# The first stage in written order, with the conditioning matrix taken in four eighth pairs of scale and shift

## The chip, the cores and the metric

The kernel runs on one core of a Trainium2 chip. The metric is device time in microseconds (us) of one execution; less is better. A core has five engines with instruction streams of their own: TensorE (PE, the matmuls), VectorE (DVE), ScalarE (ACT), GpSimd (POOL) and SyncE (SP, which here only issues DMA transfers). Each engine runs its stream in order. An instruction waits for semaphores of other engines or of DMA transfers, and everything behind it on the same engine waits with it.

## The reference

One layer of a hybrid encoder on 2048 tokens of width 1024, all float32:

```
mod = silu(c) @ w_ada + b_ada                # w_ada 1024 x 3072
shift, scale, gate = split(mod, 3)
h = RMSNorm(x) * norm_w * (1 + scale) + shift
proj = h @ w_in + b_in                       # 1024 x 4624
na = neighbourhood_attention(q, k, v, rpb) * silu(z)
ml = bidirectional chunked mLSTM(conv(q, k), v, gates) * ...
y  = concat(na, ml) @ w_out
out = RMSNorm(x + gate * y) * final_norm_w
```

The change touches `mod`, `h` and the first two column blocks of `proj`; a helper for reciprocal square roots that the later parts use too changes with it.

## The kernel before

**Numbers.** Each operand of the projection is kept as a rounded part `hi` and a remainder `lo` in a float32 form that PE multiplies in one pass. A product is three matmuls: `hi*hi`, `hi*lo`, `lo*hi`. The normed and modulated tokens stand transposed, channels on partitions, in `hhi[g]` and `hlo[g]`, one pair for each of four groups g of 512 tokens; each has eight slices k of 128 channels. A weight block is 256 columns of `w_in`. It comes as two raw halves (`raw_w`, 512 KB each); ACT writes the rounded part `whi` and POOL the remainder `wlo`. There are two slots of weights, `a` and `b`. Block 0 carries 16 more columns for the gates (`rg`).

**The first stage** is `start()`. It loads `x` of group 0, squares it on ACT (L234), takes the reciprocal root with three Newton steps (`rsqrt`, four operations a step at L1243 to L1246; for the first group on POOL, later on DVE) and scales `x` on ACT (L239). `w_ada` comes in quarters of 512 columns in the order scale 0, shift 0, scale 1, shift 1, each as eight slices of 128 rows (`wada`, 256 KB each, seven buffers). DVE multiplies every slice by a column of silu(c) and adds it up in `acc` (L249 first slice, L251 the rest). Per quarter PE sums over the partitions with four matmuls of one column against `ones` (L257). The result goes to `shT` and `gT`, the shift and the gain per channel: a copy on ACT (L260) and up to three small operations on POOL (L261, L265, L266), or one on DVE (L263).

With `gT` and `shT` of the first four slices there, `first_h` makes h of group 0: PE has transposed `x` (L273), ACT writes `hhi` and an unrounded copy `h` (L280), POOL subtracts them to `hlo` (L281). For slices 4 to 7 ACT works in two steps, `scaled` (L285) and `shifted` (L290), and DVE writes `hlo` (L291).

**The first block.** `vo_first` (L499 to L508) multiplies one slice k at a time, for all four token tiles of the group: 4 x 3 matmuls of 272 columns, into four PSUM tiles `pvo`, so that PE can start when the first slice of h is there. `vo_group` adds the biases on DVE (L524, L526), applies a sigmoid (ACT L528) and stores. With `first` unset `vo_group` does the products itself, a token tile at a time, 24 matmuls of 256 columns (`mm3`, L454 to L456). Group 0 to 2 use `vo_first` for block 0, group 3 does not; block 1 goes a tile at a time.

**What sets the order.** The work is written group by group, with generators (`next_h` as `self.chain`) that place the h of the next group (`make_h`: transposes L298, `hhi` on ACT, `h` on DVE L302, `hlo` on POOL L303) between the tiles of this one. The order in the streams then comes from a scheduler that the tile framework runs over the whole program, with its own costs; pools of buffers add waits. The streams after `start()`, blocks 2 to 5 (`tok_blocks`), convolution, mLSTM, attention and output projection, are written in the same way.

After block 5 comes the convolution stage (`pc`, first matmul at L454 from another caller). Its first products take PSUM buffers that DVE must have emptied, in L489 (`stv<-pv,brow`), which writes into staging tiles that an earlier store `d_vna` (SP, L493) must have read. SP issues that store in its stream between loads of `dec` tiles (L728), which wait for their own buffers.

## Time and profile before

| quantity | us |
|---|---|
| runs before | 1358.46, 1360.39, 1357.08 (median 1358.46) |
| the profiled execution, its own time | 1361.21 |
| its span in the trace | 1359.4 |
| mean granted TensorE clock over the span | 0.988 |
| PE busy | 1288.3 (95% of the span) |
| DVE busy | 799.0 |
| ACT busy | 532.9 |
| POOL busy | 288.9 |
| first matmul of the projection begins at | 32.21 |
| the fifth token tile of block 2 begins at | 168.09 |

The time of an execution is a little longer than its span (1361.21 against 1359.4), and a single profiled execution lies a little above the median of the runs. PE is busy nearly all the time, so a change pays if it removes time in which PE waits or runs at a lower granted clock, and the rows to look for are PE's waits and what ended them. The page's second part gives one digit per fortieth of the span, here 34 us each; the whole first stage up to block 2 lies in the first five digits.

### The profile page before, as it was taken

What the parts mean: (1) busy time and instruction counts of PE and PEld (TensorE: products, weight loads), DVE (VectorE), ACT (ScalarE), POOL (GpSimd) and SP (SyncE); (2) the same over time, 40 slices, a digit from 0 to 9 for tenths busy, and PEclk for the clock granted to TensorE, in tenths of its full rate; (3) what the DMA queues carried; (4) which work ended last, traced back from release to release, by engine and by line L of the source; (5) the groups of instructions that cost most, each with busy time, mean ns of one, the idle gap of its engine ahead of it and who ended that gap; (6) DMA issues with size and microseconds to landing.
All of it is one profiled execution on the core that took longest, in us unless ns stands there. A gap on an engine that the chain in (4) does not pass through costs nothing.

```text
span 1359.4 us, 23245 instructions
## 1 busy us (share of the span) xinstructions
PE 1288.3 (95%) x8204; PEld 1106.1 (81%) x8204; DVE 799.0 (59%) x2436; ACT 532.9 (39%) x1169; POOL 288.9 (21%) x322
## 2 busy tenths in 40 slices
PE   2989899999899999999999999899999999999996
PEld 2989899999688778788878888788877777778775
DVE  6683623111164569347677888867636676666664
ACT  4642213344432233222423333323346555555552
POOL 4454301335301011001212102212202211212121
PEclk9999999999899999999999999999999999999998
DMA  9799543599856685644665767656688986868871
GB/s 315 230 282 238 193 105 99 124 234 234 214 123 198 142 204 160 184 111 126 189 183 173 231 195 213 211 166 192 189 252 230 217 210 179 187 175 192 202 184 47
DMA packets 236359, 255.90 MB, mean 188 GB/s; under 512 B 31047, under 2 KB 192071, under 8 KB 236243
## 3 DMA queue, kind: packets, MB, share of 16 engines
q1 hardware_dynamic: 153310, 183.00, 49.8%
q0 software_dynamic: 20496, 36.21, 11.1%
q10 hardware_dynamic: 62436, 35.20, 9.2%
q8 instruction: 65, 1.06, 0.3%
q14 instruction: 52, 0.42, 0.1%
HBM read 169.81 MB, written 92.72 MB: 193 GB/s over the span
## 4 chain that ended last, share of the span: by engine, by line
PE 44%; DMA 8%; issue 6%; DVE 5%; ACT 1%; POOL 1%; SPq 0%; DVEq 0%; POOLq 0%; ACTq 0%
PE pq L892 18%; PE y L1472 9%; DMA tab<-d_t 5%; PE pT L1412 2%; PE pO L1427 2%; PE pS L1384 2%; PE px L1131 2%; PE pi L1133 2%; PE pc L454 2%; PE pc L455 2%; PE pc L456 2%; PE dc L1071 1%; DMA hlo<-d_wo 1%; PE a L1118 1%; DVE st L1055 1%
## 5 line engine op out<-in xcount | busy, mean ns | idle before, releaser
L892 PE MATMUL pq<-hhi,whi_a 128*128 128x512 f32 x512 | 208.7, 408 | 0.8 <-ACT u L797 0.8
L892 PE MATMUL pq<-hlo,whi_a 128*128 128x512 f32 x512 | 209.2, 409 | 0.0
L892 PE MATMUL pq<-hhi,wlo_a 128*128 128x512 f32 x512 | 206.9, 404 | 0.0
L892 PEld LDWEIGHTS pq<-hhi,whi_a 128*128 128x128 f32 x512 | 97.2, 190 | 17.8 <-ACT u L797 1.2
L892 PEld LDWEIGHTS pq<-hlo,whi_a 128*128 128x128 f32 x512 | 97.1, 190 | 16.2 <-issue 0.5
L892 PEld LDWEIGHTS pq<-hhi,wlo_a 128*128 128x128 f32 x512 | 97.0, 189 | 16.2
L1414 ACT ACTIVATE pt<-pT 96x384 f32<-96x384 f32 (+3 forms) x128 | 65.8, 514 | 84.7 <-PE pT L1412 81.9
L1393 ACT ACTIVATE pbuf<-pbuf,mn 128x480 f32<-128x480 f32 (+5 forms) x128 | 76.1, 596 | 54.0 <-DVE mn L1392 53.9
L1472 PE MATMUL y<-hhi,whi_a 128*128 128x512 f32 x256 | 91.6, 419 | 0.5 <-ACT whi_a L1442 0.5
L1472 PE MATMUL y<-hhi,wlo_a 128*128 128x512 f32 (+1 forms) x272 | 90.7, 399 | 0.2 <-ACT y L1479 0.2
L1392 DVE CUSTOM_DVE_ANT_0 pbuf<-pS,tab 128x480 f32<-128x480 f32 (+5 forms) x128 | 63.1, 541 | 40.3 <-PE pS L1384 29.4
L866 POOL TENSOR_TENSOR wlo_a<-rawq,whi_a 128x1024 fp32r<-128x1024 f32 x20 | 48.5, 2426 | 157.9 <-ACT whi_a L865 104.2
L1155 POOL TENSOR_TENSOR hm<-hm,ck 128x128 f32<-128x128 f32 x64 | 26.4, 412 | 253.5 <-DVE hm L1154 210.9
L1136 ACT ACTIVATE num<-px,gtile 128x129 f32<-128x129 f32 x120 | 38.2, 364 | 104.5 <-PE px L1131 83.4
L1412 PEld LDWEIGHTS pT<-ident,pbuf 128*128 128x128 f32 (+2 forms) x416 | 50.9, 137 | 29.6 <-issue 9.8
L1412 PE MATMUL pT<-ident,pbuf 128*128 128x128 f32 (+2 forms) x416 | 67.2, 275 | 8.1 <-DVE pbuf L1404 6.6
L454 PE MATMUL pvo<-whi_b,hhi 128*128 128x256 f32 x256 | 74.2, 290 | 0.6 <-DVE gates L526 0.6
L524 DVE TENSOR_TENSOR stvo<-pvo,brow 128x256 f32<-128x256 f32 x64 | 26.4, 421 | 81.6 <-PE pvo L456 62.9
L456 PE MATMUL pvo<-whi_b,hlo 128*128 128x256 f32 x256 | 72.9, 285 | 0.0
L455 PE MATMUL pvo<-wlo_b,hhi 128*128 128x256 f32 x256 | 72.8, 284 | 0.0
L739 ACT ACTIVATE dec<-dec,gtile 128x128 f32<-128x128 f32 x128 | 42.6, 393 | 56.9 <-POOL dec L732 52.9
L489 DVE TENSOR_TENSOR stv<-pv,brow 128x256 f32<-128x256 f32 x32 | 12.9, 423 | 84.4 <-PE pv L456 47.8
(301 smaller groups left out, 3484.1 us busy)
## 6 DMA issues: line engine op xcount, KB each, us to landing
ck<-d_ck SPq DMA_DIRECT2D x64, 384.5 KB
rawq<-in_w_main_dram SPq DMA_DIRECT2D x28, 512.0 KB
raw<-in_w_main_dram SPq DMA_DIRECT2D x20, 512.0 KB
d_ck<-stvo SPq DMA_DIRECT2D x16, 514.0 KB
kv<-d_ck SPq DMA_DIRECT2D x64, 128.5 KB
x<-in_x_dram SPq DMA_DIRECT2D x16, 512.0 KB
wada<-in_w_ada_dram SPq DMA_DIRECT2D x32, 256.0 KB
dec<-d_mneg SPq DMA_DIRECT2D x32, 256.0 KB
```

The costliest lines, as they stand in the source:

```text
L454: nc.tensor.matmul(ps, lhi(k), rhi(k), start=(k == 0), stop=False)
L455: nc.tensor.matmul(ps, lhi(k), rlo(k), start=False, stop=False)
L456: self.mark = nc.tensor.matmul(ps, llo(k), rhi(k), start=False, stop=(k == KT - 1))
L739: nc.scalar.activation(t[:, o, :], t[:, o, :], AF.Exp, bias=self.cols["g"][:, d, h, c : c + 1])
L866: nc.gpsimd.tensor_tensor(lo[:, :, cs], raw, hi[:, :, cs].bitcast(F32), ALU.subtract)
L892: self.mark = nc.tensor.matmul(patch_ps(ps) if patch else ps, w, self.htok(h, g, k, patch), start=(k == 0 and n == 0), stop=(k == KT - 1 a ...
L1136: nc.scalar.activation(num[:, d, :], px[:, d, :], AF.Copy, scale=self.cols["inter"][:, d, h, c : c + 1])
L1392: nc.vector.tensor_tensor_reduce(pt[:, :nk], ps, tabs[place[u]][j][:, :nk], 1.0, 3e38, ALU.add, ALU.min, mn)
L1393: nc.scalar.activation(pt[:, :nk], pt[:, :nk], AF.Exp, bias=mn, scale=-1.0, accum_out=sums[:, j : j + 1])
L1412: nc.tensor.transpose(ps[:cs, i, :], U[u][j][:, i * cs : (i + 1) * cs], self.ident)
L1414: nc.scalar.activation(t[:cs, :nch, :], ps[:cs, :nch, :], AF.Copy)
L1472: nc.tensor.matmul(y, m[:, k, :], w[k][:, cs], start=(k == 4 and n == 0), stop=(k == 3 and n == 2))
```

## The change

`start()` is run in the order in which it is written (`manual_schedule`), no longer in the scheduler's, and it is rewritten:

- `w_ada` comes in four eighth pairs e: a tile holds 256 columns of shift and the same 256 of scale for one slice of rows (128 x 2 x 256, the same 256 KB, twelve buffers). One pair gives shift and gain of two slices k = 2e and 2e+1 of h. `b_ada` is laid out to match.
- Some slices are multiplied by PE itself (`direct`: slices 1, 3, 5 of pair 0, slice 1 of pairs 1 and 2, slices 1 and 3 of pair 3); DVE sums the rest. PE adds the bias by a product with the identity that opens the group (`opened`), and the sums by four products with `ones` (`total`). `gT` is then one operation on DVE and `shT` one copy on ACT (`columns`).
- The first reciprocal root runs on DVE. The remainders of block 0's weights, of the second half of block 1's, and of h of group 0 are written by DVE, no longer by POOL.
- Twelve products into a PSUM tile `dense` that nothing reads stand in the front of PE's stream.
- All of `x` is loaded early; `x` of groups 1 and 2 lies in the memory that later holds `hhi2` and `hhi3`. `c`, `b_ada` and `norm_w` are loaded by ACT's queue.
- `vo_first` serves all four groups. It does the eight products with `hhi` for the four token tiles first and then the four with `hlo`. `make_h` of slices 0 to 4 of the next group comes in block 1 of this one, slices 5 to 7 inside the next `vo_first`.
- The fills of the attention tables are spread over the groups; a small scaling (`scale_bias`) moves back.
- `rsqrt` takes three operations per Newton step, not four, everywhere.

The diff:

```diff
-        self.start(left)
+        with self.tc.manual_schedule():
+            self.start(left)
...
+        def ada_load(e, kt):
+            w = sums[e, kt] = ada.tile([P, 2, 256], F32, tag="wada", bufs=12, name=f"wada_{e}_{kt}")
+            src = self.w_ada[kt * P : (kt + 1) * P, 0 : 2 * D].rearrange("p (a c) -> p a c", a=2)
+            nc.sync.dma_start(w, src[:, :, e * 256 : (e + 1) * 256])
+
+        def added(e, left, right):
             for j in range(4):
...
+                left_tile = left[:, j // 2, (j % 2) * P : (j % 2 + 1) * P]
+                groups[e] -= 1
+                nc.tensor.matmul(mods[e][:, j : j + 1], left_tile, right, start=False, stop=groups[e] == 0)
+
+        def opened(e):
+            groups[e] = 4 * (1 + len(direct[e]))
+            mods[e] = self.sp.tile([P, 4], F32, tag="sp", name=f"mod_{e}")
+            nc.tensor.matmul(mods[e], self.ident, bias[:, 4 * e : 4 * e + 4], start=True, stop=False)
+
+        def summed(e, kt):
+            w, c = sums.pop((e, kt)), cact[:, kt : kt + 1]
+            if kt in direct[e]:
+                added(e, w, c)
+            elif kt == 0:
+                acc[e] = ada.tile([P, 2, 256], F32, tag="acc", bufs=2, name=f"acc_{e}")
+                nc.vector.tensor_scalar(acc[e], w, c, None, ALU.mult)
             else:
...
+                nc.vector.scalar_tensor_tensor(acc[e], w, c, acc[e], ALU.mult, ALU.add)
+            next(stream, None)
+
+        def total(e):
+            added(e, acc.pop(e), self.ones[:, 0:1])
+
+        def columns(e):
+            ks, ps = slice(2 * e, 2 * e + 2), mods.pop(e)
+            nc.vector.scalar_tensor_tensor(self.gT[:, ks], ps[:, 2:4], 1.0, nw[:, ks], ALU.add, ALU.mult)
+            nc.scalar.activation(self.shT[:, ks], ps[:, 0:2], AF.Copy)
+
+        direct = {0: (1, 3, 5), 1: (1,), 2: (1,), 3: (1, 3)}
+        sums, acc, groups = {}, {}, {}
+        tps, mods = {}, {}
...
         def first_h(k):
...
+            hi = self.hhi[0][:, k, :]
...
+            return lambda: nc.vector.tensor_tensor(self.hlo[0][:, k, :], h, hi.bitcast(F32), ALU.subtract)
...
+        def loads():
+            for e in range(4):
+                for kt in range(KT):
+                    ada_load(e, kt)
+                    yield
+                if e == 1:
+                    raws.extend(self.raw_w(0, 0, (1,)))
+
+        stream = loads()
...
+        for _ in range(12):
+            next(stream)
...
+        ssq = xp.tile([P, 4], F32, tag="ssq", bufs=2, name="ssq")
+        for tt in four:
+            square(tt, ssq)
+        rst = roots(four, ssq)
+        opened(0)
+        dense = self.pp.tile([P, GT], F32, tag="pp", name="dense")
+        for kt in (0, 2):
+            summed(0, kt)
+        raws[0](nc.vector)
...
+        nc.vector.tensor_tensor(lo[:, :, 256:], rg, hi[:, :, 256:].bitcast(F32), ALU.subtract)
+        for n in range(4):
+            nc.tensor.matmul(dense, self.ident, xt[1][:, :GT], start=True, stop=True)
+        for n in range(8):
+            nc.tensor.matmul(dense[:, :256], hi[:, n % 4, :P], hi[:, n % 4, :256], start=True, stop=True)
+        for tt in four:
+            scale_x(tt, rst)
+        for kt in (4, 6, 7):
+            summed(0, kt)
+        for tt in four:
+            for k in range(2):
+                turned(k, (tt,))
+            if tt < 3:
+                summed(0, 2 * tt + 1)
+        total(0)
+        columns(0)
+        turned(2)
         first = self.vo_first(0)
...
+        for e in range(4):
+            if e < 3:
+                opened(e + 1)
+            k = 2 * e
+            rest = [kt for kt in range(KT) if e < 3 and kt not in direct[e + 1]]
+            early = [first_h(k), first_h(k + 1)]
+            for n, kt in enumerate(rest[:4]):
+                summed(e + 1, kt)
+                if n in (1, 3):
+                    early.pop(0)()
+            for fn in early:
+                fn()
+            if e == 1:
+                raws[1](nc.vector)
+            for kt in rest[4:]:
+                summed(e + 1, kt)
+            if e < 3:
+                summed(e + 1, direct[e + 1][0])
+            next(first)
+            if k + 3 < KT:
                 turned(k + 3)
...
             next(first)
...
+            if e < 3:
+                for kt in direct[e + 1][1:]:
+                    summed(e + 1, kt)
+                if k + 4 < KT:
+                    turned(k + 4)
+                total(e + 1)
+                columns(e + 1)
...
+        for tt in range(4, 8):
+            load_x(tt)
+        parts[0]()
+        parts[1](nc.vector)
...
+        for g in range(NG):
+            now = [4 * g + j for j in range(4)]
+            tiles = [tt + 4 for tt in now] if g < NG - 1 else []
+            ssq = xp.tile([P, 4], F32, tag="ssq", bufs=2, name=f"ssq_{g}") if tiles else None
+            if g:
+                for k, _ in enumerate(self.vo_first(g)):
+                    if k < 3:
+                        make_h(now, k + 5)
+                    if k == 2:
+                        self.flush()
+                        next(fills, None)
+                    if k >= 4 and tiles:
+                        square(tiles[k - 4], ssq)
+            else:
+                for tt in tiles:
+                    square(tt, ssq)
+            self.vo_group(0, 0, g, True)
+            if tiles:
+                rst = roots(tiles, ssq)
+                for tt in tiles:
+                    scale_x(tt, rst)
+            if tiles:
+                if g:
+                    self.token_tiles(g + 1)
+                self.chain = next_h(tiles)
+            else:
+                self.load_bias(2)
+                self.chain = next_w()
+            self.vo_group(1, 1, g)
+            for _ in self.chain:
+                pass
+            if tiles:
+                make_h(tiles, 4)
+            if g == 1:
+                self.scale_bias()
+            for _ in range(2 if g < NG - 1 else 0):
                 next(fills, None)
...
-                a, b = self.hhi[g][:, k, ts], self.hlo[g][:, k, ts]
-                for n, (m, w) in enumerate(((a, hi), (a, lo), (b, hi))):
-                    self.nc.tensor.matmul(ps[:, :272], m, w[:, k, :], start=(k == 0 and n == 0), stop=(k == KT - 1 and n == 2))
+                a = self.hhi[g][:, k, ts]
+                for n, w in enumerate((hi, lo)):
+                    self.nc.tensor.matmul(ps[:, :272], a, w[:, k, :], start=(k == 0 and n == 0), stop=False)
+            for o, ps in enumerate(self.firsts):
+                b = self.hlo[g][:, k, o * P : (o + 1) * P]
+                self.nc.tensor.matmul(ps[:, :272], b, hi[:, k, :], start=False, stop=(k == KT - 1))
             yield

...
             eng.tensor_tensor(t, y, y, ALU.mult)
-            eng.tensor_tensor(t, t, v, ALU.mult)
-            eng.tensor_scalar(t, t, -0.5, 1.5, ALU.mult, ALU.add)
-            eng.tensor_tensor(y, y, t, ALU.mult)
+            eng.scalar_tensor_tensor(t, t, -0.5, v, ALU.mult, ALU.mult)
+            eng.scalar_tensor_tensor(y, t, 1.5, y, ALU.add, ALU.mult)
```

What that does to the streams is shown at three places. First PE at the start of the program, before; `tp` is the transposed `x`, `mod` the PSUM tile of shift or scale, `pvo` that of block 0, `hhi_102` and `hlo_105` the two parts of h of group 0:

```order
L273 MATMUL tp_2_273<-ident,x_163 128x128
L273 MATMUL tp_0_263<-ident,x_165 128x128
L273 MATMUL tp_1_268<-ident,x_165 128x128
L273 MATMUL tp_2_273<-ident,x_165 128x128
L257 MATMUL mod_0_254<-ones,acc 128x1 x4
L257 MATMUL mod_0_278<-ones,acc 128x1 x4
L507 MATMUL pvo_0_334<-whi_a,hhi_102 128x272
L507 MATMUL pvo_0_334<-wlo_a,hhi_102 128x272
L507 MATMUL pvo_1_335<-whi_a,hhi_102 128x272
```

and with the change; `mod_219` is pair 0, `mod_299` pair 1:

```order
L270 MATMUL mod_219<-bada,ident 128x4
L358 MATMUL dense<-x_160,ident 128x512 x4
L360 MATMUL dense<-whi_a 128x256 x8
L299 MATMUL tp_0_260<-ident,x_158 128x128
L299 MATMUL tp_1_262<-ident,x_158 128x128
L265 MATMUL mod_219<-cact,wada_1_175 128x1 x4
```

```order
L265 MATMUL mod_219<-ones,acc_222 128x1 x4
L299 MATMUL tp_2_294<-ident,x_158 128x128
L299 MATMUL tp_2_294<-ident,x_160 128x128
L299 MATMUL tp_2_294<-ident,x_162 128x128
L299 MATMUL tp_2_294<-ident,x_164 128x128
L270 MATMUL mod_299<-bada,ident 128x4
L265 MATMUL mod_299<-cact,wada_1_191 128x1 x4
L582 MATMUL pvo_0_337<-whi_a,hhi_102 128x272
L582 MATMUL pvo_0_337<-wlo_a,hhi_102 128x272
L582 MATMUL pvo_1_338<-whi_a,hhi_102 128x272
```

Before, two whole quarters (scale 0 and shift 0) are summed ahead of the first product of the projection; with the change one eighth pair, the unread products, and one direct product of the second pair.

Second DVE, between the end of the first and of the second part of the conditioning, before:

```order
L249 TENSOR_SCALAR acc<-wada_0_0_230,cact 128x512
L251 SCALAR_TENSOR_TENSOR acc<-wada_0_1_233,cact,acc 128x512
L251 SCALAR_TENSOR_TENSOR acc<-wada_0_2_236,cact,acc 128x512
L251 SCALAR_TENSOR_TENSOR acc<-wada_0_3_239,cact,acc 128x512
L251 SCALAR_TENSOR_TENSOR acc<-wada_0_4_242,cact,acc 128x512
```

and with the change, one whole pair:

```order
L288 SCALAR_TENSOR_TENSOR gT<-mod_219,nw 128x2
L278 TENSOR_SCALAR acc_307<-wada_0_189,cact 128x512
L280 SCALAR_TENSOR_TENSOR acc_307<-wada_2_193,cact,acc_307 128x512
L307 TENSOR_TENSOR hlo_103<-h_0_301,hhi_102 128x512
L280 SCALAR_TENSOR_TENSOR acc_307<-wada_3_195,cact,acc_307 128x512
L280 SCALAR_TENSOR_TENSOR acc_307<-wada_4_224,cact,acc_307 128x512
L307 TENSOR_TENSOR hlo_103<-h_1_304,hhi_102 128x512
L280 SCALAR_TENSOR_TENSOR acc_307<-wada_5_227,cact,acc_307 128x512
L280 SCALAR_TENSOR_TENSOR acc_307<-wada_6_250,cact,acc_307 128x512
L280 SCALAR_TENSOR_TENSOR acc_307<-wada_7_253,cact,acc_307 128x512
L288 SCALAR_TENSOR_TENSOR gT<-mod_299,nw 128x2
```

The low parts of h now stand between the sums on DVE, and the gain is one operation on it; the sums of the next pair stand behind `gT` of this one.

Third SP ahead of the convolution, before; `d_vna` is the store from a staging tile of block 5, group 0 and then group 1, `dec` and `d_t` are other transfers:

```order
L493 DMA d_vna_60<-stv_5_0_3295 128x4x256
L728 DMA dec_23_3468<-d_mneg_62 128x512
L576 DMA d_t10_78<-d_e0_72 8x16x192
L728 DMA dec_24_3502<-d_mneg_62 128x512
L728 DMA dec_25_3536<-d_mneg_62 128x512
L576 DMA d_t10_78<-d_e0_72 8x16x192
L728 DMA dec_26_3570<-d_mneg_62 128x512
L728 DMA dec_27_3608<-d_mneg_62 128x512
L728 DMA dec_28_3642<-d_mneg_62 128x512
L493 DMA d_vna_60<-stv_5_1_3435 128x4x256
```

and with the change:

```order
L568 DMA d_vna_60<-stv_5_0_3314 128x4x256
L653 DMA d_t10_78<-d_e0_72 8x16x192
L805 DMA dec_23_3487<-d_mneg_62 128x512
L805 DMA dec_24_3521<-d_mneg_62 128x512
L805 DMA dec_25_3555<-d_mneg_62 128x512
L653 DMA d_t10_78<-d_e0_72 8x16x192
L805 DMA dec_26_3589<-d_mneg_62 128x512
L805 DMA dec_27_3627<-d_mneg_62 128x512
L568 DMA d_vna_60<-stv_5_1_3454 128x4x256
```

The second store stands behind one `dec` load less.

189 lines of the change are left out of this document (60 added, 129 removed).

## The prediction

> **What bounds the kernel now.** I read the page first, then PE's waits in the stretch up to 420 us, then the timeline of the front, then windows of the granted clock.
>
> ```profile
> span 1359.4 us, 23245 instructions
> PE   2989899999899999999999999899999999999996
> ```
>
> PE is the bound almost everywhere; only the first slice has a low digit (2 tenths of 34 us), so what a change of the first stage can be worth lies mostly there, and the next slices are at 8 and 9. The waits of PE up to the convolution say where:
>
> ```profile
> PE tp L273 <- ACT x L239: 19.5, 1, 19.5
> PE pc L454 <- DVE stv L489: 5.9, 1, 5.9
> PE pvo L507 <- ACT hhi L280: 5.1, 1, 5.1
> PE tp L298 <- DVE h L302: 3.4, 3, 1.9
> PE pvo L454 <- DVE stvo L524: 3.4, 2, 2.5
> PE pvo L507 <- ACT hhi L290: 1.6, 1, 1.6
> PE pvo L454 <- DVE gates L526: 0.6, 1, 0.6
> PE pvo L507 <- POOL hlo L303: 0.6, 1, 0.6
> PE tp L298 <- DVE x L241: 0.3, 1, 0.3
> ```
>
> (total, times, longest, in us.) 19.5 and 5.1 are the front; 8.3 (3.4 + 3.4 + 0.6 + 0.6 + 0.3) are small waits of the first two blocks; 5.9 stands before the convolution. The timeline names the front's chain:
>
> ```profile
> 11.31 5.47 DVE L251 SCALAR_TENSOR_TENSOR acc<-wada,cact,acc 128x512 f32<-128x512 f32 x7
> 14.56 0.71 POOL L1243 TENSOR_TENSOR nwt_x<-rst 128x4 f32<-128x4 f32 x1
> 18.27 4.27 ACT L239 ACTIVATE x<-x,rst 128x1024 f32<-128x1024 f32 x4 [7.27 <-POOL rst L1246]
> 25.25 1.86 PE L257 MATMUL mod<-ones,acc 128*128 128x1 f32 x8 [0.26 <-ACT gT L260]
> 30.70 0.65 POOL L261 TENSOR_TENSOR shT<-shT,bada 128x4 f32<-128x4 f32 x1
> 31.38 0.78 ACT L280 ACTIVATE hhi<-tp,shT,gT 128x512 fp32r<-128x512 f32 x1 [4.05 <-POOL shT L261]
> 32.21 0.59 PE L507 MATMUL pvo<-whi_a,hhi 128*128 128x272 f32 x1 [5.09 <-ACT hhi L280]
> 32.91 6.07 POOL L281 TENSOR_TENSOR hlo<-h,hhi 128x512 fp32r<-128x512 f32 x4 [1.56 <-ACT h L280]
> 34.49 8.19 DVE L251 SCALAR_TENSOR_TENSOR acc<-wada,cact,acc 128x512 f32<-128x512 f32 x7
> 44.20 0.95 PE L257 MATMUL mod<-ones,acc 128*128 128x1 f32 x8
> 45.19 0.16 DVE L263 TENSOR_TENSOR shT<-mod,bada 128x4 f32<-128x4 f32 x1 [2.51 <-PE mod L257]
> 46.78 2.75 DVE L291 SCALAR_TENSOR_TENSOR hlo<-hg,shT,hhi 128x512 fp32r<-128x512 f32 x4 [1.43 <-ACT hhi L290]
> 49.60 4.80 POOL L203 TENSOR_TENSOR wlo_b<-raw,whi_b 128x1024 fp32r<-128x1024 f32 x2 [2.76 <-ACT whi_b L202]
> 57.79 0.43 DVE L524 TENSOR_TENSOR stvo<-pvo,brow 128x256 f32<-128x256 f32 x1 [2.23 <-PE pvo L456]
> 60.64 0.42 DVE L524 TENSOR_TENSOR stvo<-pvo,brow 128x256 f32<-128x256 f32 x1 [2.42 <-PE pvo L456]
> 95.65 1.04 PE L298 MATMUL tp<-ident,x 128*128 128x128 f32 x8
> ```
>
> The first h waits for a shift that sat in POOL's queue until 30.70, behind the weights' remainder; PE's first product is at 32.21, the last pair of sums reaches PE at 44.20. A tile of 24 matmuls takes 60.64 - 57.79 = 2.85, so block 1 began at 57.79 - 2.85 = 54.94.
>
> **The change part by part.** All sums go against the profiled execution (1361.21, 2.75 above the median of the runs).
>
> *The first pair.* The transfers set the earliest time:
>
> ```profile
> 3.00:27.00 24.00, 6.85 (x28) 5.57 (x28) 13.83 (x22) 10.19 (x15) 7.38 (x15) 1.00 0.98 350
> ```
>
> 350 GB/s flow in the front. Before, x (four tiles of 0.52 MB) and eight slices of 0.26 MB, 4.19 MB or 12.0 us, were there at about 16.0 (the last sum, 0.75 of the row at 11.31, ends at 16.78): 4.0 us lie ahead. With the change x, half a raw block (0.52), the gate columns (0.07) and eight slices are 4.79 MB: 13.7 + 4.0 = 17.7. Then a sum of 0.7, the four column products with semaphores 0.9 (before, eight took from 44.20 to the operation on DVE at 45.19), gT 0.2: the first pair is known at C0 = 20. DVE's own queue is no later. The row at 14.56 is the fifth of twelve operations of the root some 0.77 apart, so the root began near 11.5; nine operations of 0.2 on DVE (the 201 ns of a row below) end at 13.3, and x is scaled from there instead of 18.27, four times 1.07. The first product of the projection follows at 21 to 21.5, 11 us earlier than 32.21. If everything on PE before it ran at half clock (1.86 for eight column products at 25.25 against 0.95 at 44.20) and the unread products were in the way, C0 would be 23.7; 19 is the other end. The unread products lie in the 19.5 us in which PE waited: eight matmuls of 272 columns take 1.8 even at the slower pitch,
>
> ```profile
> 35.08 0.43 PE L507 MATMUL pvo<-whi_a,hhi 128*128 128x272 f32 x1
> 35.30 0.43 PE L507 MATMUL pvo<-wlo_a,hhi 128*128 128x272 f32 x1
> 188.16 1.02 PE L439 MATMUL gp<-gsum,ones 128*1 128x512 f32 x2
> ```
>
> and four of 512 columns 2 to 4 (from 1.02 for two), so they end before x is scaled; without that cover they would cost up to 6.
>
> *The next three pairs.* PE waits for each, and DVE sets the pace: it sums six or seven slices and writes two low parts, each about 0.69 (2.75 for four at 46.78; the 1.17 of the sums at 34.49, beside POOL's row at 32.91, falls away since POOL is idle there now). Pair 1: 0.2 for gT, 0.5 for the first slice, six sums 4.1, two low parts 1.4, column products 0.9, and 0.7 for semaphores, 7.8; pair 2 has the raw half's remainder more (1.3), 9.1; pair 3 a sum less, 7.1. C3 = 20 + 24 = 44. After it the last two slices: hhi 1.0, h and hlo of both 2.7, four matmuls 0.5: the first block's products end at E0 = 48.3 against 54.94: -6.6. So 11 us at the start shrink to 6.6, because DVE now does in the front what POOL did. Bounds for E0: 46 (handovers free, C0 = 19) and 54 (C0 = 23.7, sums at 0.78, the pitch of the row at 11.31).
>
> *A new wait.* The first half of block 1's remainder is still POOL's, and is due earlier: x, weights and gate bias come behind the last slice, ACT rounds after the last h (44 + 0.2 + 2.75 + 1.05 = 48.0), POOL takes 2.4 (half of the row at 49.60): 50.4. PE, done at 48.3, waits 2.1. Queued behind that matmul is all of block 1. Bounds 0 and 4 (a second half by POOL, 2.4 more, is not in it).
>
> *From there to block 2.* Up to its fifth tile, at
>
> ```profile
> 168.09 0.39 PE L454 MATMUL pvo<-whi_a,hhi 128*128 128x256 f32 x1 [2.46 <-DVE stvo L524]
> ```
>
> PE's pure work is 20 tiles at 2.84, three groups of block 0 at 12.15 (96 matmuls of 272 columns at 2.84 / 24 x 272 / 256) and 24 sets of four transposes at 0.46 (about half of the row at 95.65): 104.3. Before it took 168.09 - 54.94 = 113.1; the 8.8 over are the 8.3 of waits above and half clock. With h of the next group made in written order, each transpose has a whole slice of products (1.5) ahead of it, and the table of waits loses L302 and L298's rows. I count the 2.1 and another 2.0 of small waits that I cannot name: 48.3 + 104.3 + 4.1 = 156.7, that is -11.4 against 168.09. Bounds of the unnamed: 0 and 8.8 (as before). In the written order ACT squares the next group's x behind block 1's weights (49.1, then four at about 1.2, to 53.9), and DVE takes root and scaling (1.8 and 2.75) to 58.5; PE wants the first transposes behind three tiles of block 1, 50.4 + 8.5 = 58.9: hidden, with 0.4 to spare. The loads of block 2's weights now stand on SP behind the wide loads and a bias row; with 1.05 and 2.4 a half they are rounded 0 to 2 ahead of their first use.
>
> *The stall before the convolution.* It costs PE 5.9 and the half clock after it:
>
> ```profile
> 344.25 0.39 SPq L493 DMA_DIRECT2D d_vna<-stv  x1
> 351.90 1.42 DVE L489 TENSOR_TENSOR stv<-pv,brow 128x256 f32<-128x256 f32 x4 [16.30 <-DMA d_vna<-stv]
> 352.50:358.20 5.70, 5.70 (x14) 4.44 (x15) 0.82 (x3) 3.87 (x12) 3.79 (x3) 0.50 1.09 287
> ```
>
> A store held back on SP until 344.25 frees DVE at 351.90. It stands behind loads that POOL and ACT release, and these hang on the gates of block 0, which come earlier with PE. One load fewer stands ahead of it now. I take 0; bounds -8.8 (5.9 and 5.7 x 0.5 both gone) and +8 (the store stays where it is in time).
>
> *Newton steps.* Four small operations become three,
>
> ```profile
> L1243 DVE TENSOR_TENSOR nwt<-rstd 128x4 f32<-128x4 f32 x48 | 9.7, 201 | 0.8
> ```
>
> 48 times 0.2 is 10 us of DVE, not of PE: those stretches show PE at 9. I take 0, bounds -2 and 0.
>
> Sum: -6.6 + 2.1 + 2.0 - 8.8 + 0 + 0 = -11.3; 1361.2 becomes 1349.9, and the median 1358.46 becomes **1347**.
>
> [...]
>
> ```profile
> 25.00:50.00 25.00, 17.86 (x107) 17.07 (x108) 19.66 (x21) 13.87 (x23) 16.59 (x15) 0.96 0.64 203
> 45.20:46.80 1.60, 0.00 (x0) 0.00 (x1) 0.17 (x2) 1.60 (x4) 1.60 (x1) 1.00 0.00 0
> 46.80:51.00 4.20, 4.17 (x20) 3.96 (x21) 2.73 (x4) 2.99 (x5) 1.44 (x2) 0.63 0.62 161
> 168.10:173.00 4.90, 4.90 (x41) 4.90 (x42) 1.35 (x4) 1.28 (x2) 0.00 (x0) 1.00 0.63 133
> ```
>
> The column behind the five engines is the granted clock. An idle stretch of 1.6 (second row) was followed by a granted clock of 0.63, one of 2.46 (the row at 168.09) by 1.00: no threshold can be read from these. [...]
>
> **The rivals.**
> *A, as summed:* 1347, own range 1341 to 1352. Chance 0.70.
> *B, swallowed before the convolution.* If the loads ahead of the store are paced by transfers and not by PE, the store keeps its time, PE waits up to 8 more: 1347 + 4 to 8, about 1353. For it: 287 GB/s in that window. Against: POOL's idle gaps in that stretch end on single loads, which were issued late. Chance 0.14.
> *C, PE cold in the front, the slower side.* PE waits in pieces, three to four times per pair, and never gets its full clock. Then a pair costs PE 24 matmuls at 0.225 (35.08 to 35.30), eight transposes at 0.26 and 9 to 13 column products at 0.23 (1.86 for eight), in all 33 us for three pairs with 1.2 of waiting each; from C0 = 23.7 that gives C3 = 57, the last slices at half pitch E0 = 63, 15 later than A: -11.3 + 15 = +3.7, about 1362. It decides where a pair takes PE over 11 us. For it: 0.63 after only 1.6. Against: the pieces are shorter than that, and the clock from 25 to 50 us, which holds several such pieces, was 0.96 as a whole. Chance 0.09.
> *D, no gain.* The pieces of 1 KB per row flow slower, or the early x and table fills crowd the slices of later pairs, so that the front ends where it ended: E0 = 54.9 and the small waits as before, 1358. Chance 0.07.
>
> **How the numbers follow.** About 0.2% (2.7 us) is what a measurement can tell from no change. A and most of B lie below 1355.7: 0.70 + 0.13 = 0.83 and some of D gives 0.84 faster; 0.07 within (D, the rest of B); 0.09 slower (C). The range takes A's unknowns and B: 1340 to 1356.
>
> **What would show it.** First product of block 0 at 20 to 24; granted clock near 1 from 25 to 48; the first block's products done at 48; a wait of about 2 of PE on POOL's remainder of slot b; the fifth tile of block 2 at 156 to 157; the wait before the convolution near 6. Wrong, if the last product of the first block comes after 54, if sums on DVE take over 0.8 each, or if that last wait has grown by the gain.

## The result and the profile after

The change made the kernel a little slower: 1366.86 us against 1359.39 (medians of 16 executions each, taken side by side). The ratio on record is 1.0047 with a 95% interval of 1.0029 to 1.0064 (the two medians alone would give 1.0055). Single executions of either kernel scatter by up to 0.6% around their median. Profiles scatter too: block 1 begins at 56.55 to 60.51 us in five profiles with the same first block, and block 4 at 249.2 to 255.3 in four profiles of the unaltered changed stage and at 250.7 to 255.4 in three of the stage before. So the causes below rest on ratios, and the profiles only say where to look; a difference of 2 or 3 us between two profiles says nothing by itself.

The page of the changed kernel, its head and PE's digits (34 us each):

```profile
span 1364.8 us, 23302 instructions
PE   6899999999798999999999999999998999999996
```

The first digit rose from 2 to 6, so the front is filled as intended, but the slice at 341 to 375 us has fallen from 8 to 7, and an 8 stands at 409 to 444 us in place of a 9. The largest of PE's waits up to 420 us (total, times, longest):

```profile
PE mod L270 <- DMA bada<-in_b_ada_dram: 10.8, 1, 10.8
PE kt L922 <- issue: 5.9, 1, 5.9
PE pvo L529 <- DVE gates L604: 5.7, 4, 2.7
PE pc L529 <- DVE stv L564: 1.2, 1, 1.2
```

The 19.5 of the front are 10.8, the 3.4 on L302 and the 5.9 before the convolution (now 1.2) have gone. In their place stands a wait of 5.9 at `kt`, the transposes of the convolution's key sums, a place that the prediction never looked at. The same views set side by side at fixed points of the program (start times of PE's instructions, from the two timelines):

| point | before | after | difference | forecast |
|---|---|---|---|---|
| first product of block 0 | 32.21 | 25.13 | -7.1 | -11 |
| first product of block 1 | 54.74 | 58.66 | +3.9 | -4.5 |
| fifth tile of block 2 | 168.09 | 167.90 | -0.2 | -11.4 |
| first product of block 4 | 255.4 | 252.3 | -3.1 | |
| first product of the convolution | 352.47 | 346.02 | -6.5 | -11.3 |
| first product behind the convolution (`pq`) | 547.25 | 553.17 | +5.9 | -11.3 |
| end of the span | 1359.4 | 1364.8 | +5.4 | -11.3 |

Two things happened. The front did not give what it should (by the scatter above, its gain up to block 4 is not clear of nothing), and a lead of 6.5 us at the start of the convolution became a lag of 5.9 at its end.

**The front.** Rows from the timeline of the changed kernel:

```profile
10.80 0.56 PE L270 MATMUL mod<-bada,ident 128*128 128x4 f32 x2 [10.80 <-DMA bada<-in_b_ada_dram]
11.22 6.59 PE L358 MATMUL dense<-x,ident 128*128 128x512 f32 x8
17.84 3.23 ACT L252 ACTIVATE x<-x,rst 128x1024 f32<-128x1024 f32 x3 [4.09 <-PE dense L358]
22.98 0.16 DVE L288 SCALAR_TENSOR_TENSOR gT<-mod,nw 128x2 f32<-128x2 f32 x1 [3.77 <-PE mod L265]
23.65 1.62 PE L265 MATMUL mod<-cact,wada 128*128 128x1 f32 x8
32.63 0.16 DVE L288 SCALAR_TENSOR_TENSOR gT<-mod,nw 128x2 f32<-128x2 f32 x1 [2.79 <-PE mod L265]
41.77 0.16 DVE L288 SCALAR_TENSOR_TENSOR gT<-mod,nw 128x2 f32<-128x2 f32 x1 [1.15 <-PE mod L265]
50.38 0.16 DVE L288 SCALAR_TENSOR_TENSOR gT<-mod,nw 128x2 f32<-128x2 f32 x1 [2.54 <-PE mod L265]
55.49 2.60 DVE L212 TENSOR_TENSOR wlo_b<-raw,whi_b 128x1024 fp32r<-128x1024 f32 x1 [1.20 <-ACT whi_b L211]
58.01 0.41 DVE L602 TENSOR_TENSOR stvo<-pvo,brow 128x256 f32<-128x256 f32 x1
58.66 0.36 PE L529 MATMUL pvo<-whi_b,hhi 128*128 128x256 f32 x1 [2.42 <-DVE gates L604]
```

The first instruction on PE opens the sum with the bias and waits for `b_ada` until 10.80: that load is issued on ACT's queue, behind an operation that waits for `c`. So the unread products start late, and the scaling of the second `x` tile, which overwrites what they read, waits for them to 17.84. The gains of the four pairs come at 22.98, 32.63, 41.77 and 50.38, each time released by PE (`mod`). DVE had then been idle for 3.77, 2.79, 1.15 and 2.54; 1.15 is little more than the eight column products that total a pair (0.95), so only the third gain waited for DVE's sums and the others for PE. Windows of the same kernel show why a pair takes PE so long (the columns are the stretch, its length, PE, PEld, DVE, ACT and POOL, the granted clock, DMA share and GB/s):

```profile
24.50:28.00 3.50, 3.50 (x17) 3.50 (x18) 3.10 (x5) 1.67 (x3) 0.00 (x0) 0.50 0.95 293
37.70:40.00 2.30, 2.18 (x19) 1.94 (x16) 2.23 (x4) 0.00 (x0) 0.00 (x0) 1.00 0.92 278
25.00:50.00 25.00, 23.29 (x145) 22.83 (x144) 17.49 (x27) 8.03 (x13) 0.00 (x0) 0.75 0.93 303
```

PE is busy nearly throughout and at half clock for much of it; over 25 to 50 us the granted clock was 0.75. The 0.96 that the prediction quotes for the same stretch of the kernel before is no measure of it. The first change in that trace's clock record comes at 37.61 and the view counts all time ahead of it as full clock, but a product of block 0 takes 0.43 there, as at 35.08 in the prediction's rows, and 0.29 behind it:

```profile
37.70 0.29 PE L507 MATMUL pvo<-whi_a,hlo 128*128 128x272 f32 x1
```

In the changed kernel the same products take 0.43 where 0.50 is recorded and 0.29 where 1.00 is. So the kernel before, too, ran at half clock up to 37.6 where its rows show a pace (products of 0.43 from 32.60 on, eight column products in 1.86 at 25.25). Taken so from 25 us on, its mean over 25 to 50 us was about 0.70, an estimate from these rows and the record behind 37.61.

**The convolution.** PE's waits from 344 to 560 us; first before:

```profile
PE pc L454 <- DVE stv L489: 5.9, 1, 5.9
PE kt L845 <- ACT acc_k L835: 3.5, 2, 3.3
```

then after:

```profile
PE kt L922 <- ACT acc_k L912: 8.4, 6, 3.7
PE kt L922 <- issue: 5.9, 1, 5.9
PE pc L529 <- DVE stv L564: 1.2, 1, 1.2
```

9.4 us of waiting became 15.5. The first wait has only moved, and with it most of the lead of 6.5: 4.7 of that lead is the shorter wait at the first product. The convolution's first products pile up in PSUM until ACT writes them out as `u`, and ACT does this behind its `dec` work, in both kernels at the same time. ACT before and after:

```profile
367.93 1.26 ACT L797 ACTIVATE u<-pc,bcol 128x512 f32<-128x512 f32 x2 [2.95 <-DMA d_ck<-dec]
```

```profile
367.87 1.26 ACT L874 ACTIVATE u<-pc,bcol 128x512 f32<-128x512 f32 x2 [2.75 <-DMA d_ck<-dec]
```

PE came 6.5 earlier and then stood for 5.9 at the first `kt`, whose sums are made from `u` (the profile names no releaser there; in two experiments below the same wait is put down to ACT's last step of `acc_k`). The rest is new, and begins with two products on DVE, the scaling of rows of the output weights by the gate (`wraw`), which SP then stores (`d_wo`). Rows of DVE and SP before:

```profile
390.66 1.28 DVE L767 TENSOR_TENSOR wraw<-wraw,gate 128x512 f32<-128x512 f32 x2
391.37 1.30 SPq L768 DMA_DIRECT2D d_wo<-wraw  x2
407.00 20.18 SPq L576 DMA_DIRECT2D d_t<-d_e  x24
```

and after, with ACT and PE at the end of the chain:

```profile
395.60 0.68 DVE L844 TENSOR_TENSOR wraw<-wraw,gate 128x512 f32<-128x512 f32 x1
401.46 0.17 DVE L879 COPY u<-u 128x2 f32<-128x2 f32 x1 [5.18 <-ACT u L874]
401.54 0.68 DVE L844 TENSOR_TENSOR wraw<-wraw,gate 128x512 f32<-128x512 f32 x1
396.31 6.27 SPq L845 DMA_DIRECT2D d_wo<-wraw  x2
402.68 0.68 SPq L926 DMA_DIRECT2D d_ck<-stk  x1
407.04 0.60 ACT L924 ACTIVATE stk<-kt 128x512 f32<-128x512 f32 x1 [5.12 <-DMA d_ck<-stk]
409.08 0.49 DVE L909 TENSOR_SCALAR acc_k<-u,cw 128x512 f32<-128x512 f32 x1 [1.84 <-DMA d_ck<-acc_k]
418.09 19.32 SPq L653 DMA_DIRECT2D d_t<-d_e  x24
431.09 1.12 PE L922 MATMUL kt<-ident,acc_k 128*128 128x128 f32 x4 [3.70 <-ACT acc_k L912]
```

Before, the two gate products stand side by side. After, the scheduler has put the second behind the copy at a later tile's edge, which waits 5.18 for an eviction. SP, in order, sits on the pair of `d_wo` stores for 6.27 instead of 1.30. Behind them stand the stores (`d_ck`) that free the staging tiles (`stk`) and sum buffers (`acc_k`), the next weights and 24 table transfers, which start 11 us later. ACT and DVE wait for those buffers, and PE for them. The source of this stage is unchanged.

### The profile page after: what moved, and what is told of

The parts are those of the page before. It is cut to its first block, busy times and chain, and to the rows that moved or that the text cites. A ratio compares the mean times of both kernels' runs of the same rounds, so it can differ in the third digit from the quotient of the medians.

```text
span 1364.8 us, 23302 instructions
## 1 busy us (share of the span) xinstructions
PE 1302.0 (95%) x8284; PEld 1116.6 (82%) x8284; DVE 776.2 (57%) x2392; ACT 536.5 (39%) x1172; POOL 261.1 (19%) x295
## 4 chain that ended last, share of the span: by engine, by line
PE 45%; DMA 8%; issue 6%; DVE 5%; ACT 1%; POOL 1%; SPq 0%; ACTq 0%; POOLq 0%; DVEq 0%
PE pq L969 18%; PE y L1548 10%; DMA tab<-d_t 4%; PE pT L1488 2%; PE pO L1503 2%; PE pS L1460 2%; PE px L1208 2%; PE pi L1210 2%; PE pc L530 2%; PE pc L531 2%; PE pc L529 2%; PE dc L1148 1%; DMA hlo<-d_wo 1%; DMA ck<-d_ck 1%; DVE st L1132 1%
```

## The experiments

**Does the convolution's order on PE cost the time?** The order of `kt` on PE had changed too, by half a tile for some. First the changed kernel with `kt` of the first ten groups held where the kernel before has it:

```diff
+            if self.pin is not None:
+                self.behind(mm, self.pin)
+                self.pin = None
...
+        if 4 * ct + g < 10:
+            self.pin = turn
```

> The change with one edit: in the convolution stage the transposes kt of the first ten conv groups are held in PE's stream where the kernel before has them (each ahead of the next pc tile). Theory O (the order of PE in the convolution stage costs what the change lost there): kt waits of 3.7 and 1.0 at 413 to 431 us go, the first product of block 7's second pair of tiles no longer slips, pq begins at about 545 to 547 instead of 553.2, the span falls by 6 to 9 us to about 1357, ratio to before 0.997 to 1.000. Rival theory T (the stage is paced by its transfers and only the earlier arrival is at fault, whatever the order): waits move but pq still begins at 551 to 554, ratio stays 1.003 to 1.006.

Measured: 1.0051 (1.0022 to 1.008), nothing won. The wait moved on to one of 8.21 at 402.61, and SP shows the same hold as in the change, in the same place of its stream:

```profile
390.07 6.27 SPq L850 DMA_DIRECT2D d_wo<-wraw  x2
```

The counterpart is the kernel before with three `kt` placed late, as the change has them:

```diff
+        place = {4: (9, 9), 5: (9, 21), 6: (10, 13)}.get(4 * ct + g)
+        if place:
+            self.hooks.setdefault(place, []).append(turn)
```

> The kernel before with one edit: three of the transposes kt (the fifth to the seventh group) stand in PE's stream where the change has them, some 1.4 tiles later. Theory O: the raw weights of the next block and the 24 table transfers behind them on SP are issued some 10 us later than 406, PE waits in kt appear, pq begins 5 to 9 us later than 547.3, ratio to before 1.004 to 1.007. Theory T: pq within 1.5 us of 547.3, ratio 0.999 to 1.001.

Measured: 1.0018 (1.0 to 1.0037); the stretch from the first product of the convolution to `pq` took 196.4 against 194.8. So PE's order of `kt` alone does not cost the 12 us that the stage lost; the second interval leaves room for a small part of it.

**Does the order on all engines?** The two kernels exchange the order of this stage: the lists of the edit name 832 PE, 241 DVE, 87 ACT, 165 SP and 7 POOL instructions, and each is held behind its predecessor in the other kernel's stream. The computation is the same.

```diff
+CONV_ORDER = {
...
+        for row in CONV_ORDER.values():
+            row = [kept[base + n] for n in row if base + n in kept]
+            for ahead, behind in zip(row, row[1:]):
+                self.behind(behind, ahead)
```

> The change, with all instructions of the convolution stage (PE, VectorE, ScalarE, GpSimd and SyncE) held in the order in which the kernel before has them. Theory O (the scheduler wrote the convolution stage in a worse order after the change, above all two products by the gate on VectorE two tiles later, behind which SyncE's stores wait): from the first product of that stage to the first of the attention projection (pq) it takes 195 to 199 us instead of 204 to 208, the time falls by 5 to 8 us, ratio to before 0.996 to 1.001. Rival T (the stage is paced by transfers that do not come earlier): the waits are elsewhere, pq begins at 547 or later as in the change, ratio 1.003 to 1.006.

> The kernel before, with all instructions of its convolution stage held in the order that the change has. Theory O: the stage takes 5 to 9 us longer than the 194.8 of before, ratio to before 1.003 to 1.007. Rival T: the stage takes 194 to 197, ratio 0.999 to 1.001.

Measured: the changed kernel with the order of before 0.9962 (0.9939 to 0.9985), the kernel before with the order of the change 1.0087 (1.0057 to 1.0116). So the order is worth 0.0085 in one kernel and 0.0087 in the other, each give or take 0.003: some 12 us. The rest of the change wins 0.4%. The stage from the first product to `pq` went from 207.2 to 192.2 us in the one and from 194.8 to 204.2 in the other. Counted from block 4, so that a wait moved to or from the first product does not count, the profiles give 14.4 less and 3.3 more; the 12 us rest on the ratios. As both kernels were held in this way, holding the order is not itself the cause. PE from 400 to 440 us, changed kernel, then with the order of before:

```profile
400.00:440.00 40.00, 34.34 (x145) 26.71 (x144) 26.08 (x44) 11.88 (x18) 4.73 (x2) 0.91 0.81 198
```

```profile
400.00:440.00 40.00, 40.00 (x184) 32.40 (x183) 20.99 (x40) 11.74 (x19) 4.77 (x2) 1.00 0.77 197
```

The 5.7 of idle time have gone, and the granted clock is 1.00 instead of 0.91. The other kernel shows the reverse; it kept its front, and its waits at `kt` from 344 to 560 us are

```profile
PE kt L86 <- ACT acc_k L86: 14.4, 7, 6.1
```

with no wait at the first product: its 5.9 moved to the first `kt` (6.1), the same move as in the change.

**Which engine's?** Only DVE's 241 instructions in the order of before:

```diff
+CONV_ORDER = {
+    'DVE': [...]
```

> The change with only VectorE's instructions of the convolution stage held in the order of before; PE, ScalarE and SyncE keep what the scheduler wrote for the change. If VectorE's order (the products by the gate two tiles later) is what cost the stage its time, it takes 195 to 199 us from the first pc to the first pq and the ratio to before is 0.994 to 0.999. If the place of the transposes kt on PE or the order of the stores on SyncE is needed too, it takes 201 to 208 and the ratio is 1.001 to 1.006.

Measured: 1.0008 (0.9981 to 1.0036), between the change and the full order, and between the two forecasts; the stage took 198.2, as the first of them had it. SP's hold is gone though SP's stream was not touched:

```profile
389.52 0.93 SPq L82 DMA_DIRECT2D d_wo<-wraw  x2
411.92 19.56 SPq L82 DMA_DIRECT2D d_t<-d_e  x24
```

and behind 400 us PE waits 1.9 at `kt` instead of 8.4. A wait of 6.1 at the first `kt` stays. By the ratios DVE's order explains 0.0039 of the 0.0085, about half, with intervals that leave room for a small part or for most; whether the other half is that first wait or the order of the other four engines is not separated.

**What held the front back?** Four runs on the changed kernel, each with its own convolution order as scheduled; in all four the second `d_wo` store on SP comes 6 us behind the first, as in the change. Without the unread products:

```diff
-        for n in range(4):
-            nc.tensor.matmul(dense, self.ident, xt[1][:, :GT], start=True, stop=True)
-        for n in range(8):
-            nc.tensor.matmul(dense[:, :256], hi[:, n % 4, :P], hi[:, n % 4, :256], start=True, stop=True)
```

> The change without its twelve unread products (four of 512 and eight of 256 columns). Theory H (they hold up the front: x_1 cannot be scaled until the last of them has read it): x_1 is scaled at about 13.7 instead of 17.84, the first pair's gain comes at 19.5 to 20.5 instead of 22.98, and block 1 begins 2 to 3 us earlier than 58.66 unless PE is slower for want of them. Rival W (they keep PE's clock up): the clock is at half from the first transposes on and block 1 begins at 60 or later.

Measured: 1.0049 (1.0024 to 1.0074), as the change; block 1 at 58.32. PE transposes `x` from 13.95 on, 4.6 earlier, but the column products now take as long as at half clock. The first gain comes at 22.25 instead of 22.98, short of the 19.5 to 20.5 forecast, and nothing is left of it where block 0 begins (24.96 against 25.13):

```profile
14.43 1.71 PE L265 MATMUL mod<-cact,wada 128*128 128x1 f32 x8
```

Eight column products take 1.71 here and 0.95 with the unread products ahead. Then `b_ada` and `norm_w` loaded ahead of the operation that waits for `c`:

```diff
         nc.scalar.dma_start(cact, self.cT)
+        nc.scalar.dma_start(bias, self.b_ada)
+        nc.scalar.dma_start(nw, self.norm_w)
```

> The change with the loads of b_ada and norm_w issued on ACT's queue ahead of the silu of c and not behind it. Theory L (PE's first instruction waits for b_ada until 10.8, and the unread products and x_1's scaling wait behind it): b_ada is there by 5 to 7, the unread products end 4 to 5 us earlier than 18.6, the first pair's gain comes at 20 to 21, block 1 begins 2 to 3 us earlier than 58.66. Rival (the last w_ada slice of the first pair, summed at 19.2, bounds it anyway, or PE's half clock takes it back): gain at 22 or later, block 1 within 1 us of 58.66.

Measured: 1.0036 (1.0014 to 1.0059). The bias is there 5.0 earlier and the first gain comes at 19.55, 3.4 earlier, but block 1 begins at 58.06, only 0.6 earlier than in the one profile of the change:

```profile
5.80 0.56 PE L270 MATMUL mod<-bada,ident 128*128 128x4 f32 x2 [5.80 <-DMA bada<-in_b_ada_dram]
```

The later pairs took 9.78, 9.95 and 10.50 here against 9.65, 9.14 and 8.61. But that is not the early bias: the run with the old convolution order, whose first block is that of the change, has 9.67, 9.95 and 10.53 and begins block 1 at 60.51. So what the early gain is worth at block 1 cannot be told from these profiles. Third, 14 more unread products of 256 columns around the sums of each pair, to keep the clock up:

```diff
+                unread(spare, 6)
                 total(e + 1)
+                unread(spare, 8)
```

> The change with 14 more unread products of 256 columns per pair of the front: six ahead of the four column products that total a pair, eight behind them, where PE waits for sums and for the gain. Theory A (the column products and the short waits let PE's clock fall to half for 3 to 9 us at a time, and then PE is the bound of a pair): the matmuls of block 0 keep the full pitch of 0.126 in most of the front, a pair takes 7.5 to 8.5 instead of 8.6 to 9.7, block 1 begins 2 to 5 us earlier than 58.7. Rival D (VectorE's sums are the bound, PE's clock does not matter, or more work does not raise it): block 1 begins at 58 or later.

Measured: 1.0089 (1.0055 to 1.0122), against theory A. The clock fell all the same, at 41.02, and block 1 began at 59.79. PE in the stretch ahead of the fall and behind it (length, PE busy, clock, DMA share, GB/s):

```profile
37.61:41.02 3.41, 2.19 (x19) 1.00 0.89 268
41.02:44.44 3.42, 3.42 (x19) 0.50 0.89 245
```

The bounds of these stretches are no accident. In the profiles of both kernels the times at which the recorded clock changes lie 3.41 us or a multiple of it apart; in the changed kernel they are, up to block 1, 23.91, 30.74, 34.15, 37.57, 44.39, 47.81, 51.22 and 54.63. PE's products into `pvo` alone in stretches of that grid:

```profile
20.50:23.91 3.41, 0.00 (x0) 1.00 1.04 325
23.91:27.33 3.42, 2.20 (x10) 0.50 0.94 272
27.33:30.74 3.41, 2.90 (x13) 0.50 1.09 365
30.74:34.15 3.41, 0.63 (x5) 1.00 1.09 348
34.15:37.57 3.42, 3.07 (x12) 0.50 0.88 265
```

The clock fell behind the first and the fourth of them, although PE was busy for 3.41 and 2.95 us there, with transposes and products of one to four columns above all, and it rose behind the third and the fifth. Counted over the profiles of both kernels up to 560 us, with all products of 256 and more columns: the 11 falls follow stretches with at most 1.09 us of such products, no stretch with less than 1.59 kept full clock, and the 11 rises follow stretches with 2.91 or more (four with 0.33 to 2.58 did not yet bring it back). In the filled run the stretch ahead of the fall holds 1.20 of them (eight unread products) and a wait of 1.29 for DVE's sums. So the filling stood in the wrong place or was too little. Two waits in the prediction fit as well: the 1.6 idle at 45.20 lie in a stretch with 1.02 of such products, and the 2.46 ahead of 168.09 are spread over two stretches with 1.72 and 2.64. This is read from the records; no run was made to try it.

Fourth, all slices summed on DVE, none on PE:

```diff
-        direct = {0: (1, 3, 5), 1: (1,), 2: (1,), 3: (1, 3)}
+        direct = {0: (), 1: (), 2: (), 3: ()}
```

> The change with every slice of w_ada summed by VectorE and none multiplied by PE: seven groups of four column products (0.8 us each at full clock, 1.6 at half) less on PE, seven sums of 0.69 more on VectorE. Theory A (PE at half clock bounds a pair): a pair gets shorter by 0.5 to 1.5 us and block 1 begins 1 to 4 us earlier than 58.7. Rival D (VectorE bounds it): each pair 0.7 longer, block 1 begins 2 to 4 us later.

Measured: 1.004 (1.0013 to 1.0067), block 1 at 58.01. DVE's idle time ahead of the later gains is 1.15, 1.30 and 1.15 here, so now its sums bound every pair: the bound went from PE to DVE and little was won. None of the four runs moved block 1 out of the 56.55 to 60.51 of the unaltered first block.

**The two waits behind it.** All from here on with the convolution in the order of before. The second half of block 1's remainder written by DVE only after the first block's bias adds; and the first product of the gate row, which waits for a transfer on DVE ahead of bias adds of group 3, held behind the last of these. The first:

```diff
-        parts[1](nc.vector)
+        parts[1](nc.vector, 0)
...
+            if g == 0:
+                parts[1](nc.vector, 2)
```

(0 writes the rounded part alone, 2 the remainder alone.)

> The change with the convolution stage in the order of before and the second half of block 1's remainder written by VectorE behind block 0's bias adds. The wait before block 1 falls from 2.4 to under 1.3, and PE may wait inside block 1's first tile for that half, 0 to 1 us; if GpSimd's first half ends later than the bias adds, the wait stays at 2.

The second:

```diff
-                    nc.vector.tensor_scalar(a, t, cact[:, kt : kt + 1], None, ALU.mult)
+                    self.behind(nc.vector.tensor_scalar(a, t, cact[:, kt : kt + 1], None, ALU.mult), self.last_gate)
```

> The change with the convolution stage in the order of before and the first product of the gate row held behind the last gate add of block 0 on VectorE. The wait of PE at the last group's block 1 falls from 2.7 to under 1 and the half clock behind it goes, so block 2 begins 3 to 4 us earlier after block 1's first tile than without it; if VectorE was busy there with other work anyway, the wait stays above 2.

Measured: 0.994 (0.9913 to 0.9968) for the first, with no wait at block 1 (54.91), and 0.9928 (0.9904 to 0.9953) for the second, without the wait that the change has there (rows of the change):

```profile
142.41 0.75 DVE L506 SCALAR_TENSOR_TENSOR gsum<-ga,cact,gsum 128x512 f32<-128x512 f32 x1 [1.21 <-DMA ga<-in_w_ada_dram]
143.74 0.55 PE L529 MATMUL pvo<-whi_b,hhi 128*128 128x256 f32 x1 [2.69 <-DVE gates L604]
```

Both, with the early bias (the three diffs together):

> The change with the convolution stage in the order of before and three edits of the first stage: b_ada and norm_w loaded ahead of the silu, the second half of block 1's remainder written by VectorE behind the four bias adds of block 0 and not ahead of them, and the first product of the gate row on VectorE held behind the last gate add of block 0. If the waits of 2.4 before block 1 and of 2.7 (and 1.4 of half clock behind it) before the last group's block 1 are what the traces name, both go, the fifth tile of block 2 comes 4 to 7 us earlier than in the same order without these edits (about 169.9), and the ratio to before is 0.990 to 0.995, under the 0.9962 of that kernel. If another wait takes their place (PE on block 1's remainder, then on the transposes), the ratio stays at 0.995 to 0.998.

Measured: 1343.91, 0.9916 (0.9885 to 0.9947). Against the 0.9962 of the old order alone the first edit is within the noise of the ratios, the second at its edge and the three together just beyond it. Last, in addition the low parts of h of group 0 on POOL again, and then all slices summed on DVE as well (the diff of `direct` above):

```diff
-            return lambda: nc.vector.tensor_tensor(self.hlo[0][:, k, :], h, hi.bitcast(F32), ALU.subtract)
+            nc.gpsimd.tensor_tensor(self.hlo[0][:, k, :], h, hi.bitcast(F32), ALU.subtract)
+            return lambda: None
```

> The mended kernel (convolution in the order of before and the three edits of the first stage) with the low part of group 0's h written by GpSimd again, as before the change; in the forecast VectorE's two low parts (1.4 us a pair) lengthen the front. If VectorE sets the pace of the pairs, a pair gets up to 1.4 shorter and block 1 begins 2 to 5 us earlier than the 54.9 to 55.9 of the kernels in which its remainder is late. If PE at half clock sets the pace, pairs keep 8.6 to 10 and block 1 begins within 1.5 us of that. If GpSimd's slower subtractions (about 1.3 to 1.5 each) become what PE waits for, block 1 begins later and PE shows waits on GpSimd's hlo.

> The kernel of e12_low_pool with every slice of w_ada summed by VectorE and none multiplied by PE: per pair one or two groups of column products less on PE (0.8 each at full clock, 1.6 at half), as many sums of 0.69 more on VectorE, so VectorE has about as much as in the mended kernel and PE less. If PE at half clock sets the pace of the pairs, block 1 begins 2 to 4 us earlier than in e12_low_pool and in the mended kernel. If VectorE does, it begins 2 to 3 us later than in e12_low_pool. If both lie close together, neither edit moves block 1 by more than 1.5 us.

Measured: 1343.68, 0.9901 (0.987 to 0.9931), and 0.9914 (0.989 to 0.9939); block 1 at 54.97 and 56.59, against 55.87 with the three edits alone: differences within the scatter of profiles. The low parts did not relieve DVE. Its sums are slower while POOL writes them; three with the low parts on DVE, and six partly beside POOL:

```profile
23.90 2.32 DVE L322 SCALAR_TENSOR_TENSOR acc<-wada,cact,acc 128x512 f32<-128x512 f32 x3
20.07 6.48 DVE L322 SCALAR_TENSOR_TENSOR acc<-wada,cact,acc 128x512 f32<-128x512 f32 x6
```

Between the first gain and the last the sums took 0.75 each with the low parts on DVE, and with them on POOL 1.08 on average in the row of six and 1.14 in one of five (5.70 at 39.52); DVE was busy for 20.36 us from 20 to 50 us instead of 18.48. So the first of the two runs cannot tell what less work on DVE would bring. In the second every later gain comes 1.15 behind DVE's last sum, so there DVE sets the pace. The 0.9901 is the lowest ratio of the study, but its interval overlaps those of the two runs beside it. All three kernels beat both the kernel before and the change. Block 1 begins in them about where it does in the kernel before (54.74); the gain lies behind it, up to block 2 (94.9 us in the first of the last two against 102.2) and beyond.

## Why the prediction was wrong

**The step that failed** is the end of the sum, -6.6 + 2.1 + 2.0 - 8.8 + 0 + 0: it stops at the stall before the convolution and puts everything behind it at nothing, as moving with PE. The streams were compared up to the second `d_vna` store and not behind it. The scheduler had rewritten the convolution stage: it took 207.2 us instead of 194.8, and by the two exchanges of ratios that order costs some 12 us. It turned a gain of 0.4% into a loss of 0.5%. No rival named it; the loss was given 0.09 for another reason (C). Of the 16.7 us between the forecast and the measured span, 4.8 were there at the convolution's first product and 12.4 came in that stage.

The first stage failed as well, and less visibly. With the old order behind it the ratio of 0.9962 gives about 1354, not 1347, and by the fifth tile of block 2 the change had won 0.2 us, not 11.4.

By the terms of the sum:

- *The first block, -6.6.* It measured 56.2 for the end of its products against 48.3 forecast and 54.9 before: a loss of 1.3. The first gain came at 22.98, not 20 (+3.0); the pairs took 9.65, 9.14 and 8.61 against 7.8, 9.1 and 7.1 (+3.4); the tail after the last gain 5.8 instead of 4.3 (+1.5). The pair whose sum was DVE's (9.1) was right, and sums took 0.75 as bounded; what was missing is PE, which the first, second and fourth gain waited for and which ran at half clock for part of every pair (0.50 for 6.83, 3.42 and 3.42 us of the three). No row shows the 0.7 that each pair was given for semaphores; in a pair of the change PE waits 0.46 for `shT` and DVE 0.54 for `h`. The half clock is rival C's mechanism, and it decided earlier than C said: C wanted PE over 11 us per pair, while 9.65 was enough to pass DVE's 7.8. C's size (63) was not reached. C was set aside because of the 0.96 from 25 to 50 us, which does not hold (see the front). What the 3.0 at the start cost further on is not shown.
- *The new wait, 2.1.* Measured 2.42, but the culprit was wrong. POOL's half was in time; DVE's half (2.60 at 55.49, partly beside POOL's half, which ran from 54.59 to 57.00) stood ahead of the bias adds that free the PSUM tiles. Written behind them it took 1.21 and the wait was gone.
- *To the fifth tile of block 2, 104.3 + 2.0.* Measured 167.90 - 58.66 = 109.2, against 113.4 before. The named waits of L302 went as forecast; the surplus of 2.9 fits the wait of 2.69 behind the gate row and the half clock that followed it (0.50 from 143.38 to 146.79): with that wait gone the stretch took 105.3.
- *The stall before the convolution, 0.* Rival B was partly true. The wait at the first product shrank from 5.9 to 1.2, and 5.9 came back at the first `kt`, since ACT's `dec` work ended at the same time as before in these two profiles. What was called one wait is the meeting of PE with a chain that did not move with PE here. It can move: with the two waits mended ACT's first `u` came at 354 to 358, not 368.
- *Newton steps, 0.* Nothing contradicts it; no run tried them alone. From `pq` to the end the kernels with the changed steps took 807 to 817 us and the three with the old ones 812 to 814.
- *The price of the unread products.* The row at 188.16 was read as two products of 512 columns; it is one, as every product of plain float32 operands leaves two records here (four of L265 leave eight). So four of them would be 4 at that pace, the upper end of the 2 to 4 given, and they took 6.59.

Right were the sign of the change without the rewritten order (0.9962), the root on DVE (10.42 to 12.57 by its rows, forecast 11.5 to 13.3) and the unread products as no cost, though for the wrong reason: they lie in no free time, they delay the transposes by 4.6 and pay that back by the pace (eight column products in 0.95, without them 1.71). The sign is partly luck: the gain was put into the front, where the profiles show none clear of the scatter. With the old order it shows from block 4 to `pq`, 286.5 us against 291.9 and 293.9 in two profiles of the kernel before and of the one with late `kt`.

**Left open:** what the other half of the convolution's 12 us is; where the 0.4% without it comes from, beyond these profiles; and whether a front with more wide products in every 3.41 us would keep its clock and be faster. That idle time alone lowers the clock is ruled out: it fell behind a stretch in which PE was busy throughout (3.41 of 3.41 us).

## What to carry to other kernels

Where a scheduler orders the whole program, a change at its start is also a change of every later stage: compare the streams to the end before summing, and pin the order of the stages that are not meant to change. In a stage that is left alone, the place of a pair of small instructions on one engine can matter, if an in-order store queue stands behind both and buffers hang on what is queued there; here restoring that engine's order gave back about half. A stall at which PE meets a chain of another engine may keep its end when PE comes earlier; it then only shows under another name. And before a row of one profile is set against another, ask how far the same code moves between two profiles.

## What was not expected of the hardware

In the profiles of both kernels the granted clock changed only on a grid of 3.41 us, and in the changed kernel it fell to 0.50 behind a stretch that PE spent busy with transposes and products of one to four columns (3.41 of 3.41 us at 20.50). Behind which stretches it fell and rose is counted under the filled run. Where in the stream the clock rises differs between executions: the run with the late remainder has the change's stream up to the last gain, and the products of block 0 quicken in it at 45.2 to 45.4 (0.43 at 43.60, 0.29 at 45.42), in the change at 47.7 to 47.9 (0.43 at 47.45, 0.29 at 47.87). These two took pairs of 9.18, 9.14 and 8.51 and of 9.65, 9.14 and 8.61, and the run with the old convolution order, with the same stream there, 9.67, 9.95 and 10.53; that this is the reason for the scatter is likely and not shown.

VectorE's sums took 1.08 on average in a row of six partly beside GpSimd's subtractions and 0.77 in one of three without them, and its subtraction of 1.21 took 2.60, partly beside one. The four products of 512 columns against the identity took 6.59 us at the start.
